# Shift and scale of the first layer as matrix products in four column groups, with two Q and K tiles run between the parts of V

## The chip, the cores and the metric

The kernel runs on one core of a Trainium2 chip. The metric is the device time of one execution in microseconds (us); of several runs the median counts.

## The reference

Two blocks of two layers each, on 256 tokens of width 1024, all in float32. Each layer computes six modulation vectors from a conditioning vector `c`, modulates a normed input, attends (or convolves), and runs a gated feed-forward. Only the start of the very first layer is touched by the change:

```python
c_act = jax.nn.silu(c)                                       # (1, 1024)
mod = jnp.einsum('bd,dm->bm', c_act, w_mod[i]) + b_mod[i]    # (1, 6 * 1024)
sh_a, sc_a, gt_a, sh_f, sc_f, gt_f = jnp.split(mod, 6, axis=-1)
h = rmsnorm(x, g_mix_pre[i]) * (1.0 + sc_a) + sh_a           # (256, 1024)
qkv = jnp.einsum('bsd,de->bse', h, w_qkv[i])                 # q, k, v: 1024 columns each
o = stick_breaking_attention(q, k, v)                        # 16 heads of 64
```

## The kernel before

Every product of activations with weights keeps float32 accuracy by a split: a weight chunk of 128x1024 comes in as `w`, ScalarE casts it to `wh` (the CAST rows), VectorE subtracts to get the rest `wl`, and three matmuls (`wh` with `hh`, `wl` with `hh`, `wh` with `hl`) make one product (`mm3`). A chunk that is loaded is 1 MB (two such halves) and lies in a slot of the class K8; there are three (`SLOTS`). SyncE issues all loads, in one queue.

The program is first recorded, then ordered by a list scheduler (`Rec.schedule`, with a planner's own costs), and put out in that order, engine by engine; on the chip each engine works through its own list in order and waits where an operand is not there.

The first layer begins with `first_values`. The width 1024 of the input is cut into eight tiles of 128 (`kt`), and these into four parts `q` of two tiles. For part `q`:

- `mods(q)` loads four 512 KB tiles `w` of `w_mod` (transposed: one output per partition) and VectorE reduces each against `c_act`, which stands on all partitions in `rows` (`dot`, the CUSTOM_DVE rows with their accumulator reads). `scale_of` makes (1 + scale) times gain. The columns are `msh_a` and `msc_a`.
- `first_tps` transposes the normed input `xn` of the part into `tps` (TensorE); VectorE (first tile) and ScalarE (second) apply scale and shift into `hf`, and that is split into `h0h`, `h0l` (parts 0 and 1) or `h1h`, `h1l` (parts 2 and 3).
- V is summed in four PSUM banks `acc`: 24 matmuls of 128x512 for each part, which this text calls V0 to V3. They need the part's `h` and the two halves of the part's V chunk.

After V3, `attention1` goes through eight tiles of Q and K (`project_t`, PSUM tile `qkps`, 48 matmuls of 128x256 each; QK0, QK1, ... here), then scores `z`, weights, transposes `atp` and outputs `op`. The reductions for the later modulation vectors run beside them on VectorE (`bg`). The order of the loads around the change: the four parts' `w_mod` tiles and V chunks in turn, then QK0, QK1, the first chunk of `w_o`, QK2.

Of the kernel before, what the change touches and what calls it, by code (L numbers as in the profile page):

```python
# [263 lines left out]
class Rec:  # L264
# [19 lines left out]
    def record(self, eng, fn, args, kw):  # L284
        op = Op()
        op.i, op.eng, op.fn, op.args, op.kw = len(self.ops), self.ENGINES[eng], fn, args, kw
        op.outs, op.deps, op.tiles, op.dma, op.act = [], {}, [], 0, 0
        outs = [kw[k] for k in ("out", "accum_out") if isinstance(kw.get(k), VAP)]
        ins = [v for k, v in kw.items() if k not in ("out", "accum_out") and isinstance(v, VAP)]
        pos = [a for a in args if isinstance(a, VAP)]  # L290
        if pos and "out" not in kw:
            outs.append(pos[0])
            pos = pos[1:]
        ins += pos
        if fn == "matmul" and not kw["start"]:
            ins.append(outs[0])
        for v in ins:
            self.access(op, v, False)
        for v in outs:
            self.access(op, v, True)  # L300
        if fn == "matmul" and kw["start"]:
            v = outs[0]
            for w in v.t.writes:
                if w[3] is not op and w[1] < v.parts[1] and w[2] > v.parts[0]:
                    op.deps.setdefault(w[3], 1)
        if self.after is not None:
            op.deps.setdefault(self.after, 1)
        for t in op.tiles:
            t.ops.append(op)
        op.cost = self.cost(op, outs, ins, args, kw)  # L310
        self.ops.append(op)
# [271 lines left out]
class Builder:  # L583
# [44 lines left out]
    def setup(self):  # L628

        nc, io = self.nc, self.io  # L630
        self.mhalf = self.const.tile([P, 16], F32, tag="mhalf", name="mhalf")
        nc.gpsimd.memset(self.mhalf, -0.5)
        self.cact = self.const.tile([P, 24], F32, tag="cact", name="cact")
        nc.sync.dma_start(out=self.cact, in_=self.io["vecs"][:, 0:24])
        self.eye = self.const.tile([P, P], F32, tag="eye", name="eye")
        nc.sync.dma_start(out=self.eye, in_=io["consts"][:, 0:P])
        self.vec = self.const.tile([P, NVEC], F32, tag="vec", name="vec")
        nc.sync.dma_start(out=self.vec[:, 0 : self.FIRST], in_=self.io["vecs"][:, 0 : self.FIRST])
        nc.scalar.activation(out=self.cact, in_=self.cact, func=AF.Silu)
        self.cb = {0: self.on_all_rows(self.cact[:, 0:8])}  # L640

    def setup_x(self):
# [311 lines left out]
    def values(self):  # L954
# [12 lines left out]
        self.bg(0.2)  # L967
        return self.evict_v(acc)

    def first_values(self):  # L970

        nc, io = self.nc, self.io
# [5 lines left out]
        def mods(q):  # L978
            for k in range(2):
                f = q * 2 + k  # L980
                i = len(self.plan)
                self.plan.append([("w_mod", 0, None, 1, a * D + f * P, D) for a in range(2)])
                for a, kind in enumerate(("sh_a", "sc_a")):
                    w = self.sb.tile([P, D], F32, name="w0")
                    nc.sync.dma_start(out=w, in_=io["wst"][i][:, a * D : (a + 1) * D])
                    if f + a == 0:
                        self.setup_x()
                    self.dot(w, self.cb[0], 0, 0, kind, f)
                self.scale_of(0, 0, "sc_a", f, 1)

        mods(0)
        xn = [self.normed(self.x[t], None, self.xe[t]) for t in range(2)]
        for q in range(4):
            w = self.w.load()
            tps = self.first_tps(xn, q)
            for k in range(2):
                kt = q * 2 + k
                a, b = self.modcols["sc_a"][:, kt : kt + 1], self.modcols["sh_a"][:, kt : kt + 1]
                h = self.sb.tile([P, 2, P], F32, name="hf")
                if k == 0:  # L1000
                    nc.vector.tensor_scalar(out=h, in0=tps[:, k], scalar1=a, scalar2=b, op0=ALU.mult, op1=ALU.add)
                else:
                    nc.scalar.activation(out=h, in_=tps[:, k], func=AF.Identity, scale=a, bias=b)
                hh, hl = self.hm(self.h, kt)
                nc.scalar.copy(hh, h)
                nc.vector.tensor_tensor(out=hl, in0=h, in1=hh.bitcast(F32), op=ALU.subtract)
            if q < 3:
                mods(q + 1)
# [4 lines left out]
        nc.after = nc.ops[-1]  # L1013
        self.setup_rest()
        nc.after = None
        return self.evict_v(acc)

    def first_tps(self, xn, q):
# [113 lines left out]
    def attention1(self, i):  # L1132
        nc = self.nc
        stick = i == 0
        vs = self.first_values() if stick else self.values()
        cum = None
        if stick:
            self.cprod = [self.sb.tile([P, 386], F32, tag=f"cp{k}", name=f"cp{k}") for k in range(2)]
            for cp in self.cprod:
                nc.gpsimd.memset(cp[:, 128:129], 1.0)  # L1140
                nc.gpsimd.memset(cp[:, 385:386], 1.0)
        else:
            cum = self.forget_cum()
        wo = Stream(self, [(("w_o", i, j * P, 2, 0, D),) for j in range(0, KT, 2)])
        qk, a, os_, w2 = {}, {}, {}, {}
        for it in range(KT + 2):
            if it < KT:
                w = self.w.take()
                ps = self.pmm.tile([P, 512], F32, tag="mm", name="qkps")
                for m in range(2):  # L1150
                    self.project_t(ps[:, m * S : (m + 1) * S], w[m], self.h)
# [409 lines left out]
    def run(self):  # L1561
# [93 lines left out]
```

## Time and profile before

| | us |
|---|---|
| median of 3 runs | 1354.19 (1352.99 to 1358.27) |
| the profiled execution, its own time | 1356.83 |
| its span, first to last instruction | 1355.0 |
| TensorE busy in the span | 1318.0 (97%) |
| VectorE busy | 1083.6 (80%) |
| ScalarE busy | 716.2 (53%) |

The profile is of one execution; its own time is 2.6 us above the median. A timeline row has the start, the duration, the engine, the operation with its output and inputs, the shape, how many alike were merged, and in brackets how long the engine had been idle and what ended that. A matmul's end is modelled, so the pace of TensorE is read from start to start of rows. PE is TensorE, PEld its weight loads, DVE VectorE, ACT ScalarE, SP SyncE. L544 is the line of the helper that records every operation, so rows are told apart by their tiles.

### The profile page before, as it was taken

The page shows a single profiled execution, that of the slowest core. Times are in us where ns is not written, and L with a number is a line of the kernel's source. Part 1 is how long each engine was busy: PE and PEld are TensorE (multiplying, and loading weights), DVE is VectorE, ACT ScalarE, POOL GpSimd, SP SyncE. Part 2 cuts the span into 40 slices and gives each one's busy share as a digit, 9 for nine tenths or more (in the row PEclk, how much of TensorE's full clock was granted, in tenths as well). Part 3 has the DMA queues.
Part 4 walks back from the last instruction along what each step waited for, and adds up shares of the span by engine and source line. Part 5 has one row for each costly group of instructions (what it writes and reads, how often), then busy time and mean ns, then how long its engine had stood idle before and what let it go on. Part 6 is the DMA issues. An engine that isn't in the chain of part 4 may idle for free.

```text
span 1355.0 us, 21985 instructions
## 1 busy us (share of the span) xinstructions
PE 1318.0 (97%) x8776; PEld 1178.4 (87%) x8776; DVE 1083.6 (80%) x1825; ACT 716.2 (53%) x1249; POOL 72.4 (5%) x102
## 2 busy tenths in 40 slices
PE   5999899999999999999999999899999999999998
PEld 3788799999898799999988777799999899899997
DVE  6888989899898499999799998886776898855542
ACT  3565655555656484556454567754444545744430
POOL 0000100000100000001033112100000000000000
PEclk9999999999999999999999999899999999999999
DMA  9857578887666256667544641576776688455520
GB/s 360 316 211 272 194 280 321 330 313 293 239 252 252 89 184 260 267 252 270 206 161 173 226 154 63 189 304 254 280 269 260 231 300 309 181 193 186 187 95 32
DMA packets 45320, 311.84 MB, mean 230 GB/s; under 512 B 5280, under 2 KB 5664, under 8 KB 8864
## 3 DMA queue, kind: packets, MB, share of 16 engines
q1 hardware_dynamic: 45216, 310.42, 61.3%
q8 instruction: 69, 1.13, 0.3%
q14 instruction: 35, 0.29, 0.1%
HBM read 309.35 MB, written 1.05 MB: 229 GB/s over the span
## 4 chain that ended last, share of the span: by engine, by line
PE 90%; DVE 6%; ACT 2%; issue 1%; DMA 0%; POOL 0%; SPq 0%; ACTq 0%; POOLq 0%
PE gu L544 34%; PE acc L544 30%; PE qkps L544 7%; PE fp L544 4%; PE cu L544 3%; PE z L544 2%; PE bb L544 2%; PE qps L544 2%; DVE w L544 2%; PE op L544 1%; DVE wl L544 1%; PE dop L544 1%; PE tps L544 1%; PE kc L544 1%; PE atp L544 1%
## 5 line engine op out<-in xcount | busy, mean ns | idle before, releaser
L544 DVE TENSOR_TENSOR wl<-w,wh 128x1024 fp32r<-128x1024 f32 x392 | 470.8, 1220 | 77.9 <-ACT wh L544 54.7
L544 ACT CAST wh<-w 128x1024 fp32r<-128x1024 f32 x392 | 402.4, 1049 | 98.8 <-DMA w<-in_wst_dram 56.7
L544 DVE CUSTOM_DVE_ANT_0 w<-w,rows,vec 128x1024 f32<-128x1024 f32 x192 | 242.4, 1278 | 9.9 <-DMA w<-in_wst_dram 9.6
L544 PE MATMUL gu<-h1h,wh 128*128 128x256 f32 x640 | 181.3, 283 | 0.0
L544 PE MATMUL gu<-h1h,wl 128*128 128x256 f32 x640 | 181.2, 283 | 0.0
L544 PE MATMUL gu<-h0h,wl 128*128 128x256 f32 x640 | 181.1, 283 | 0.0
L544 PE MATMUL gu<-h1l,wh 128*128 128x256 f32 x640 | 181.1, 283 | 0.0
L544 PE MATMUL gu<-h0l,wh 128*128 128x256 f32 x640 | 181.1, 283 | 0.0
L544 PE MATMUL gu<-h0h,wh 128*128 128x256 f32 x640 | 180.9, 283 | 0.0
L544 PE MATMUL acc<-wh,yh 128*128 128x512 f32 x352 | 137.6, 392 | 0.0
L544 PE MATMUL acc<-wl,yh 128*128 128x512 f32 x352 | 137.5, 391 | 0.0
L544 PE MATMUL acc<-wh,yl 128*128 128x512 f32 x352 | 135.3, 389 | 0.0
L544 PEld LDWEIGHTS gu<-h0l,wh 128*128 128x128 f32 x640 | 122.6, 192 | 2.2
L544 PEld LDWEIGHTS gu<-h0h,wh 128*128 128x128 f32 x640 | 122.5, 192 | 2.3
L544 PEld LDWEIGHTS gu<-h1l,wh 128*128 128x128 f32 x640 | 122.8, 192 | 0.1
L544 PEld LDWEIGHTS gu<-h1h,wh 128*128 128x128 f32 x640 | 122.8, 192 | 0.1
L544 PEld LDWEIGHTS gu<-h1h,wl 128*128 128x128 f32 x640 | 122.8, 192 | 0.0
L544 PEld LDWEIGHTS gu<-h0h,wl 128*128 128x128 f32 x640 | 122.6, 192 | 0.0
L544 DVE TENSOR_TENSOR y<-s,gu 128x256 f32<-128x256 f32 x80 | 33.5, 418 | 76.2 <-ACT s L544 76.2
L544 ACT ACTIVATE s<-gu 128x256 f32<-128x256 f32 x40 | 15.4, 385 | 138.0 <-PE gu L544 138.0
L544 PEld LDWEIGHTS acc<-wh,yl 128*128 128x128 f32 x352 | 66.1, 188 | 14.3
L544 PEld LDWEIGHTS acc<-wh,yh 128*128 128x128 f32 x352 | 66.3, 188 | 12.2 <-ACT yh L544 0.2
(364 smaller groups left out, 2690.4 us busy)
## 6 DMA issues: line engine op xcount, KB each, us to landing
w<-in_wst_dram SPq DMA_DIRECT2D x284, 1024.0 KB, 4.9
w<-in_wst_dram SPq DMA_DIRECT2D x16, 512.0 KB, 11.4
x<-in_x_dram SPq DMA_DIRECT2D x2, 512.0 KB, 6.6
cx<-in_ctx_dram SPq DMA_DIRECT2D x2, 512.0 KB, 6.3
out_dram<-x SPq DMA_DIRECT2D x1, 512.0 KB, 2.6
out_dram<-x SPq DMA_DIRECT2D x2, 256.0 KB, 2.0
cst<-in_consts_dram SPq DMA_DIRECT2D x1, 264.0 KB, 5.2
smalls<-in_smalls_dram SPq DMA_DIRECT2D x1, 256.0 KB, 5.2
```

The costliest lines, as they stand in the source:

```text
L544: fn(*[real(a) for a in op.args], **{k: real(v) for k, v in op.kw.items()})
```

## The change

Four things change, all in the first layer's first stage.

1. The 16 reductions of `mods` leave VectorE. `first_mods(q)` loads the same bytes of `w_mod`, now untransposed (rows of `c` on the partitions, 256 columns of shift and 256 of scale), and TensorE multiplies: for each of the four tiles, four matmuls with 32 equal columns of `c_act` as weights, each into its own 32 partitions of one PSUM tile `gv`. ScalarE copies `gv` to `gvs`; four matmuls against the column `four` (1 at partitions 0, 32, 64, 96) add the four groups and turn the row into columns; VectorE adds the bias and makes the scale, two columns at a time.
2. TensorE's instructions in this stage stand in the order in which the code writes them (`nc.serial`), not in the scheduler's.
3. QK0 and QK1 are run in parts between V's parts (`BETWEEN`, `project_part`), and their weight chunks are loaded between V's: V0, V1, QK0, V2, QK1, V3.
4. `setup_rest` (two small loads of constants) stands ahead of V2's chunk in the load queue instead of behind V3.

```diff
+        if self.serial is not None and op.eng == "PE":
+            if self.serial:
+                op.deps.setdefault(self.serial[-1], 1)
+            self.serial = [op]
...
+    def first_mods(self, q):
...
+        ps = self.pmm.tile([P, 512], F32, name="gv")
+        for a in range(2):
+            for kt in range(KT):
+                h, g = kt // 4, kt % 4
+                nc.tensor.matmul(
+                    ps[32 * g : 32 * g + 32, a * S : (a + 1) * S], lhsT=self.cact[:, kt : kt + 1].to_broadcast([P, 32]),
+                    rhs=ws[a, h][:, g * S : (g + 1) * S], start=h == 0, stop=h == 1,
+                )
+        gv = self.sb.tile([P, 512], F32, name="gvs")
+        nc.scalar.copy(gv, ps)
+        yield
+        for c in range(4):
+            nc.tensor.matmul(ps[:, c : c + 1], lhsT=gv[:, c * P : (c + 1) * P], rhs=self.four, start=True, stop=True)
...
+    BETWEEN = {1: ((0, (0, 1, 2, 3)),), 2: ((0, (4, 5)), (1, (0, 1, 2, 3, 4, 5))), 3: ((0, (6, 7)), (1, (6, 7)))}
...
             w = self.w.take(w)
             for t in range(2):
                 for k in range(2):
                     self.acc_mm(acc, t, self.hx(self.h, t, q * 2 + k), w[k], q + k == 0, q + k == 4)
...
+            if q < 3:
+                next(mods[q + 1])
+                tps = self.first_tps(xn, q + 1)
+            parts = [(j, kt) for j, kts in self.BETWEEN.get(q, ()) for kt in kts]
...
+            for n, (j, kt) in enumerate(parts):
+                if n == 2 and q < 3:
+                    next(mods[q + 1])
+                self.project_part(self.early_qk[j], qkw[j], (kt,))
...
-                specs += self.value_specs(i) + self.qk_specs(i)
+                v, qk = self.value_specs(i), self.qk_specs(i)
+                specs += v + qk if i else [v[0], v[1], qk[0], v[2], qk[1], v[3]] + qk[2:]
```

The instructions move on three engines. First TensorE between V0 and V1. Before, the last matmuls of V0 (`wl_239`, `wh_213`) are followed at once by V1's (`wh_246`, `wl_254`):

```order
L544 MATMUL acc_217<-wl_239,h0h_200 128x512
L544 MATMUL acc_217<-wh_213,h0l_204 128x512
L544 MATMUL acc_219<-wl_239,h0h_200 128x512
L544 MATMUL acc_219<-wh_213,h0l_204 128x512
L544 MATMUL acc_211<-wh_246,h0h_200 128x512
L544 MATMUL acc_215<-wh_246,h0h_200 128x512
L544 MATMUL acc_217<-wh_246,h0h_200 128x512
```

Now (V0's last two, then the products for part 1, its transposes, the four sums, then V1's first three, with `wh_267` and `wl_280`):

```order
L551 MATMUL acc_248<-wl_228,h0h_214 128x512
L551 MATMUL acc_248<-wh_222,h0l_224 128x512
L551 MATMUL gv_258<-w_44_111,cact_83 32x256 x4
L551 MATMUL gv_258<-w_45_113,cact_83 32x256 x4
L551 MATMUL gv_258<-w_46_115,cact_83 32x256 x4
L551 MATMUL gv_258<-w_47_117,cact_83 32x256 x4
L551 MATMUL tps_277<-eye_85,xn_173 128x128
L551 MATMUL tps_277<-eye_85,xn_181 128x128
L551 MATMUL gv_258<-four_143,gvs_286 128x1 x4
L551 MATMUL acc_220<-wh_267,h0h_214 128x512
L551 MATMUL acc_220<-wl_280,h0h_214 128x512
L551 MATMUL acc_220<-wh_267,h0l_224 128x512
```

The products for part 1 stand behind all of V0, and nothing stands between the four sums and V1. Between V1 and V2, V2 and V3 the pieces of QK0 and QK1 fill that place.

Second, VectorE at the same place. Before, a reduction (the rows named ISA) and the rest of V0's chunk (`wl_239`) are followed by the scale and by `hf`:

```order
L544 ISA w_44_117,raw_176<-w_44_117,rows_148,vec_91 128x1024
L544 ISA raw_176 128x1
L544 TENSOR_TENSOR wl_239<-w_37_109,wh_213 128x1024
L544 SCALAR_TENSOR_TENSOR msc_a_184<-raw_176,vec_91 128x1
L544 TENSOR_SCALAR hf_242<-tps_169,msc_a_184,msh_a_156 128x256
L544 TENSOR_TENSOR wl_254<-w_49_119,wh_246 128x1024
L544 TENSOR_TENSOR h0l_204<-hf_242,h0h_200 128x2x128
```

Now the two biased sums, then the two rests of QK0's chunk (`wl_300`, `wl_305`) on either side of the scale, then `hf`:

```order
L551 TENSOR_TENSOR msh_a_204<-gv_258,vec_91 128x2
L551 TENSOR_TENSOR raw_206<-gv_258,vec_91 128x2
L551 TENSOR_TENSOR wl_300<-w_58_121,wh_291 128x1024
L551 SCALAR_TENSOR_TENSOR msc_a_208<-raw_206,vec_91 128x2
L551 TENSOR_TENSOR wl_305<-w_58_121,wh_302 128x1024
L551 TENSOR_SCALAR hf_307<-tps_277,msc_a_208,msh_a_204 128x256
L551 TENSOR_TENSOR h0l_224<-hf_307,h0h_214 128x2x128
```

The reductions are gone, and both rests of QK0 stand ahead of the `hf` that V1 waits for. Third, ScalarE. Before, the cast of V2's first half (`wh_289`) stands ahead of the casts of part 2's `h`:

```order
L544 CAST h0h_200<-hf_257 128x2x128
L544 CAST wh_289<-w_61_129 128x1024
L544 CAST h1h_299<-hf_292 128x2x128
L544 ACTIVATE hf_304<-tps_174,msh_a_156,msc_a_184 128x256
```

Now, from the copy of part 1's products to the cast of V2's second half (`wh_291`, `wh_302` are QK0's halves, `wh_406`, `wh_412` V2's):

```order
L551 COPY gvs_286<-gv_258 128x512
L551 CAST wh_291<-w_58_121 128x1024
L551 CAST wh_302<-w_58_121 128x1024
L551 CAST h0h_214<-hf_307 128x2x128
L551 ACTIVATE hf_312<-tps_277,msh_a_204,msc_a_208 128x256
L551 CAST h0h_214<-hf_312 128x2x128
L551 COPY gvs_361<-gv_341 128x512
L551 CAST h1h_400<-hf_393 128x2x128
L551 ACTIVATE hf_402<-tps_358,msh_a_204,msc_a_208 128x256
L551 CAST wh_406<-w_63_237 128x1024
L551 CAST h1h_400<-hf_402 128x2x128
L551 CAST wh_412<-w_63_237 128x1024
```

The casts of QK0's halves now stand behind the copy of part 1's products, and V2's first cast stands behind part 2's `h`. From the first feed-forward on the order is the same as before, but for a few rows at its start.

## Rows read from the trace of the kernel before

**Rows 1.** The page's first line and its busy line: us busy, share of the span, instructions, engine by engine.

```profile
span 1355.0 us, 21985 instructions
PE 1318.0 (97%) x8776; PEld 1178.4 (87%) x8776; DVE 1083.6 (80%) x1825; ACT 716.2 (53%) x1249; POOL 72.4 (5%) x102
```

**Rows 2.** The view by stretches of 10 us: the stretch and its length, then busy us (and instructions) of PE, PEld, DVE, ACT and POOL, then TensorE's granted clock (1.00 is full speed), the busy share of the DMA engines and GB/s.

```profile
30.00:40.00 10.00, 7.38 (x32) 5.55 (x30) 10.00 (x18) 3.97 (x6) 0.00 (x0) 1.00 1.01 410
40.00:50.00 10.00, 7.38 (x26) 5.91 (x26) 8.50 (x14) 4.80 (x9) 0.00 (x0) 0.83 0.56 205
50.00:60.00 10.00, 10.00 (x78) 9.69 (x77) 6.94 (x8) 7.86 (x11) 0.00 (x0) 1.00 0.85 326
```

**Rows 3.** What TensorE waited for: us in total, times, the longest. The first two rows from the stretch 0 to 60 us, the last two from 60 to 170 us (the largest of five there, 4.7 us together).

```profile
PE acc L544 <- DVE wl L544: 7.1, 3, 2.6
PE acc L544 <- ACT wh L544: 2.4, 1, 2.4
...
PE fp L544 <- ACT h0h L544: 1.9, 4, 0.7
PE tps L544 <- DVE u L544: 1.8, 1, 1.8
```

**Rows 4.** Timeline: V's first matmuls; QK0's first; QK1's last and the first scores.

```profile
18.39 2.07 PE L544 MATMUL acc<-wh,h0h 128*128 128x512 f32 x4 [2.38 <-ACT wh L544]
...
51.75 0.28 PE L544 MATMUL qkps<-h0h,wh 128*128 128x256 f32 x1
...
63.14 0.28 PE L544 MATMUL qkps<-h1h,wl 128*128 128x256 f32 x1
63.35 0.49 PE L544 MATMUL z<-qk 64*128 64x128 f32 x4
```

**Rows 5.** Timeline of ScalarE: the first casts of the chunks of V1, V2 and V3, each started by its load's landing.

```profile
24.01 1.04 ACT L544 CAST wh<-w 128x1024 fp32r<-128x1024 f32 x1 [4.42 <-DMA w<-in_wst_dram]
31.61 1.04 ACT L544 CAST wh<-w 128x1024 fp32r<-128x1024 f32 x1 [2.97 <-DMA w<-in_wst_dram]
39.19 1.05 ACT L544 CAST wh<-w 128x1024 fp32r<-128x1024 f32 x1 [2.19 <-DMA w<-in_wst_dram]
```

**Rows 6.** Timeline of TensorE: float32 products with 64 columns of weights (`op`), in two column groups in turn. Each call of the code leaves two rows. First all four calls of a pair of heads together (two of 256 columns, two of 128), then one call of 256 columns alone; the row behind each shows when the next matmul began.

```profile
73.77 0.87 PE L544 MATMUL op<-at,v 128*64 128x256 f32 x8
74.57 0.39 PE L544 MATMUL qkps<-h0l,wh 128*128 128x256 f32 x1
...
83.22 0.65 PE L544 MATMUL op<-at,v 128*64 128x256 f32 x2
83.80 0.39 PE L544 MATMUL qkps<-h0h,wl 128*128 128x256 f32 x1
```

**Rows 7.** The same for the whole array: four transposes of 128x128, and four float32 products with 128 columns of weights and 128 columns streamed (`dop`), each with the row behind it; last, eight weight loads for transposes early in the span.

```profile
780.33 0.66 PE L544 MATMUL dtp<-eye,p 128*128 128x128 f32 x4
780.74 0.49 PE L544 MATMUL acc<-wh,h0h 128*128 128x512 f32 x1
...
782.00 1.15 PE L544 MATMUL dop<-dv,dat 128*128 128x128 f32 x8
782.90 0.47 PE L544 MATMUL acc<-wh,h0l 128*128 128x512 f32 x1
...
11.22 1.57 PEld L544 LDWEIGHTS tps<-eye,xn 128*128 128x128 f32 x8 [6.28 <-DVE xn L544]
```

**Rows 8.** Timeline: V matmuls at full clock, three and three; V matmuls at half clock.

```profile
47.65 0.86 PE L544 MATMUL acc<-wh,h1h 128*128 128x512 f32 x3
48.34 0.85 PE L544 MATMUL acc<-wl,h1h 128*128 128x512 f32 x3
...
43.75 0.63 PE L544 MATMUL acc<-wl,h1h 128*128 128x512 f32 x1
44.18 0.63 PE L544 MATMUL acc<-wh,h1l 128*128 128x512 f32 x1
```

**Rows 9.** Prices of the small steps, from the timeline: ScalarE's copy of 512 columns out of PSUM, VectorE's rest of a half chunk, scale and `hf`, ScalarE's cast of `hf` and its own `hf`; and the page's group of the reductions (busy us, mean ns).

```profile
4.53 0.59 ACT L544 COPY rows<-rowps 128x512 f32<-128x512 f32 x1 [1.84 <-PE rowps L544]
33.10 1.22 DVE L544 TENSOR_TENSOR wl<-w,wh 128x1024 fp32r<-128x1024 f32 x1
34.24 0.15 DVE L544 SCALAR_TENSOR_TENSOR msc_a<-raw,vec 128x1 f32<-128x1 f32 x1
34.31 0.54 DVE L544 TENSOR_SCALAR hf<-tps,msc_a,msh_a 128x256 f32<-128x256 f32 x1
34.88 0.41 ACT L544 CAST h1h<-hf 128x256 fp32r<-128x256 f32 x1 [2.22 <-DVE hf L544]
35.19 0.56 ACT L544 ACTIVATE hf<-tps,msh_a,msc_a 128x256 f32<-128x256 f32 x1
...
L544 DVE CUSTOM_DVE_ANT_0 w<-w,rows,vec 128x1024 f32<-128x1024 f32 x192 | 242.4, 1278 | 9.9 <-DMA w<-in_wst_dram 9.6
```

**Rows 10.** The view by stretches again (columns as in rows 2), around a wait of TensorE from 40.1 to 42.7 us.

```profile
34.30:40.20 5.90, 5.73 (x24) 4.43 (x24) 5.90 (x13) 3.13 (x5) 0.00 (x0) 1.00 0.99 406
40.20:42.70 2.50, 0.00 (x0) 0.00 (x0) 2.50 (x8) 0.04 (x1) 0.00 (x0) 1.00 0.09 33
42.70:46.20 3.50, 3.47 (x8) 2.82 (x9) 3.10 (x5) 2.96 (x6) 0.00 (x0) 0.51 0.67 225
```

**Rows 11.** The page's DMA issues: the 1 MB chunks, KB each, median us from issue to landing.

```profile
w<-in_wst_dram SPq DMA_DIRECT2D x284, 1024.0 KB, 4.9
```

More of the change, by code (lines that the diff above doesn't have):

```diff
@@ L639, in setup @@
         nc.scalar.activation(out=self.cact, in_=self.cact, func=AF.Silu)
+        self.four = self.const.tile([P, 1], F32, tag="four", name="four")
+        nc.vector.tensor_reduce(
+            out=self.four, in_=self.eye.rearrange("p (a d) -> p a d", a=4)[:, :, 0], axis=AX.X, op=ALU.add
+        )
         self.cb = {0: self.on_all_rows(self.cact[:, 0:8])}
@@ L968, in values @@
         return self.evict_v(acc)
+    def first_mods(self, q):
+        nc = self.nc
+        i = len(self.plan)
+        self.plan += [[("w_mod", 0, 0, KT, a * D + q * S, S)] for a in range(2)]
+        ws = {}
+        for a in range(2):
+            for h in range(2):
+                ws[a, h] = self.sb.tile([P, D], F32, name="w0")
+                nc.sync.dma_start(out=ws[a, h], in_=self.io["wst"][i + a][:, h * D : (h + 1) * D])
+                if q + a + h == 0:
+                    self.setup_x()
+        yield
+        ps = self.pmm.tile([P, 512], F32, name="gv")
+        for a in range(2):
+            for kt in range(KT):
[3 more added lines that the diff above has]
+                    rhs=ws[a, h][:, g * S : (g + 1) * S], start=h == 0, stop=h == 1,
+                )
+        gv = self.sb.tile([P, 512], F32, name="gvs")
+        nc.scalar.copy(gv, ps)
+        yield
+        for c in range(4):
+            nc.tensor.matmul(ps[:, c : c + 1], lhsT=gv[:, c * P : (c + 1) * P], rhs=self.four, start=True, stop=True)
+        f = 2 * q
+        for a, (kind, out) in enumerate((("sh_a", self.modcols["sh_a"]), ("sc_a", self.raw["sc_a"]))):
+            nc.vector.tensor_tensor(
+                out=out[:, f : f + 2], in0=ps[:, 2 * a : 2 * a + 2], in1=self.v(f"b00{kind}", f, 2), op=ALU.add
+            )
+        self.scale_of(0, 0, "sc_a", f, 2)
+        yield
@@ new lines, in first_h @@
+    def first_h(self, tps, q):
+        nc = self.nc
+        for k in range(2):
+            kt = q * 2 + k
+            a, b = self.modcols["sc_a"][:, kt : kt + 1], self.modcols["sh_a"][:, kt : kt + 1]
+            h = self.sb.tile([P, 2, P], F32, name="hf")
+            if k == 0:
+                nc.vector.tensor_scalar(out=h, in0=tps[:, k], scalar1=a, scalar2=b, op0=ALU.mult, op1=ALU.add)
+            else:
+                nc.scalar.activation(out=h, in_=tps[:, k], func=AF.Identity, scale=a, bias=b)
+            self.split_to(self.hm(self.h, kt), h)
@@ L976, in first_values @@
         self.raw["sc_a"] = self.sb.tile([P, 8], F32, name="raw")
[L978 to L991, printed above, removed]
+        mods = [self.first_mods(q) for q in range(4)]
+        nc.serial = []
+        next(mods[0])
+        next(mods[0])
+        w = self.w.load()
         xn = [self.normed(self.x[t], None, self.xe[t]) for t in range(2)]
+        tps = self.first_tps(xn, 0)
+        next(mods[0])
+        self.first_h(tps, 0)
+        qkw, self.early_qk = {}, {}
         for q in range(4):
[L994 to L1006, printed above, removed]
+            if q in (1, 2):
+                late = self.w.load()
             if q < 3:
-                mods(q + 1)
+                next(mods[q + 1])
+                nextw = self.w.load()
+            if q == 2:
+                self.setup_rest()
             w = self.w.take(w)
@@ L1012, in first_values @@
                     self.acc_mm(acc, t, self.hx(self.h, t, q * 2 + k), w[k], q + k == 0, q + k == 4)
[L1013 to L1015 removed]
+            if q < 3:
+                next(mods[q + 1])
+                tps = self.first_tps(xn, q + 1)
+            parts = [(j, kt) for j, kts in self.BETWEEN.get(q, ()) for kt in kts]
+            if q in (1, 2):
+                qkw[q - 1] = self.w.take(late)
+                self.early_qk[q - 1] = self.pmm.tile([P, 512], F32, name="qkps")
+            for n, (j, kt) in enumerate(parts):
+                if n == 2 and q < 3:
+                    next(mods[q + 1])
+                self.project_part(self.early_qk[j], qkw[j], (kt,))
+            if q < 3:
+                if len(parts) <= 2:
+                    next(mods[q + 1])
+                self.first_h(tps, q + 1)
+                w = nextw
+        nc.serial = None
         return self.evict_v(acc)
@@ L1147, in attention1 @@
             if it < KT:
[L1148 to L1151, printed above, removed]
+                ps = self.early_qk.pop(it, None)
+                if ps is None:
+                    w = self.w.take()
+                    ps = self.pmm.tile([P, 512], F32, tag="mm", name="qkps")
+                    for m in range(2):
+                        self.project_t(ps[:, m * S : (m + 1) * S], w[m], self.h)
                 qk[it] = self.sb.tile([P, 512], F32, tag="qk", name="qk")
```

14 lines of the change are left out of this document (12 added, 2 removed).

## Prediction

> **What bounds the kernel now.** The page first [rows 1]: TensorE is busy for 1318.0 us of the span of 1355.0. Only 37 us are idle, and the question is where. The stretches [rows 2] answer it: TensorE has 7.38 us of work in each of the stretches 30 to 40 and 40 to 50, and 10.00 from 50 to 60. VectorE is full in the first of them, and the DMA engines move 410 GB/s. The waits [rows 3] name the rest: until 60 us TensorE waits 7.1 us for VectorE's `wl` and 2.4 for the first cast; between 60 and 170 us it waits 4.7 us in all, and the two largest items, 1.9 and 1.8, belong to the step from the attention to the feed-forward. So the span is TensorE's own work, plus holes nearly all of which lie in the first 50 us. What the change is worth is therefore one difference: when TensorE has V, QK0 and QK1 behind it. Before, V begins at 18.39, QK0 at 51.75, and QK1 is done at 63.35 [rows 4]. In those 45 us it has 96 V matmuls, three of them in 0.69 us at full clock [rows 8], that is 0.23 each or 21.9 us (at 0.228), and 96 QK matmuls from 51.75 to 63.35, 0.12 each or 11.5. The remaining 11.5 us are holes and half clock. The change can fill at most these, and has to pay out of them for all that it adds to TensorE.
>
> **What leaves VectorE.** Sixteen reductions of 1.28 us [rows 9], 20.5 us. They set the pace of V before: each of the three waits for `wl` had reductions ahead of it in VectorE's queue. The added small steps there (two sums and a scale for each part, at most 0.15 each [rows 9]) are under 2 us.
>
> **When the data land.** The same 8 MB of `w_mod` are loaded. Three chunk times, 24.01, 31.61 and 39.19 [rows 5], lie 3 MB apart, so 1 MB takes 2.53 us. Before V1's chunk the queue is unchanged: V1 lands at 24.0, and part 0's four `w_mod` tiles, 4 MB ahead of it, at 24.0 - 10.1 = 13.9. From there on QK0 lands at 26.5, part 2's tiles at 31.6, part 3's at 36.7, then the two small loads (0.46 MB), V2 at 40.4, QK1 at 43.0, V3 at 45.5. Part 1's tiles are there at 21.5. Of these only part 0's tiles hold up the path below.
>
> **What TensorE gains in work.** One part's products are 16 calls of 256 columns in four groups of 32. No row of before shows four groups; the nearest show two [rows 6]. A call of 256 columns alone holds the array from 83.22 to 83.80, 0.58. Two of 256 and two of 128 in two groups take 73.77 to 74.57, 0.80. With c for a call of 256, half of it for 128, and s for going in and out: side by side 1.5c + s = 0.80 and c + s = 0.58, so c = 0.44 and s = 0.14. One after the other would be 3c + s = 0.80, so c = 0.11; but four whole-array calls of 128 columns take 0.90 [rows 7], 0.22 each, which is c = 0.44. So two groups do run side by side. Bounds for a part: four at a time 4 x 0.44 + 0.14 = 1.9; two at a time 8 x 0.44 + 0.14 = 3.7; one at a time 7.2. I take 1.9, since the rows show no loss at two.
>
> The Trainium skill, "TensorEngine Tiling (Array Packing)", Tiling Modes, has four independent tiles for 128 rows and 32 columns, but says that changing the mode drains the engine; the trace agrees with the second in the 0.14. The skill's "TensorE: Matmul & The Clock Gate", Part 3, gives 2.38 times for three column tiles; by that share, an estimate from this page, a part would take 2.4 and the sum below would be 1.4 us higher.
>
> The four sums are weight loads with one column streamed: at most the 0.90 of four whole-array calls [rows 7], at least the 0.41 of four transposes [rows 7]; I take 0.90, since the loads are of the same kind. The four transposes, 0.41, now stand on the path too.
>
> **The path, part by part.** Ends of one engine and starts of the next lie within 0.05 us in the rows; I add 0.2 for the last result of TensorE.
>
> Start of V0. The last tile lands at 13.9; the last four products, at the half pace of the start (V's first four matmuls take 2.07 [rows 4], where three take 0.69 later [rows 8]), 0.9 and 0.2: 15.0. Copy 0.59: 15.6, while the transposes run until 15.9. The four sums are eight weight loads at that pace, 1.57 [rows 7], and 0.2: 17.7. Sums and scale 0.4, `hf` 0.54, cast 0.41 [rows 9]: V0 begins at 19.2, 0.8 later than before. Its first half needs `wl`, which stands behind `hf` (1.22, third matmul at 20.3), runs at half pace (0.43 each [rows 8]) and waits for the second half's `wl` until 22.4; at full pace from there, V0 ends at 26.5. That is 7.3 us where the matmuls alone are 5.5.
>
> Between V0 and V1. Products 1.9 and 0.2: 28.6. Copy: 29.2. Four sums 0.9 and 0.2: 30.35. Now VectorE's order bites: after the two biased sums it must make the rest of QK0's first half, whose cast stands behind the copy on ScalarE (30.3), 1.14 from start to start [rows 9], then the scale, then the second rest, 1.14, then `hf` 0.54: 33.5. Cast: V1 begins at 34.0. TensorE stands still for 3.8 us after the four sums; its longest wait for `wl` before was 2.6 [rows 3]. A hole of 2.6 us, 40.1 to 42.7, left it at a granted clock of 0.51, the 1.2 GHz of its two levels, for about 3.2 us; another, which ended at 34.3, did not, as the 1.00 of the stretch behind it shows [rows 10]. I count the lower level after V1's hole: 1.6 us lost. V1 is 5.5 + 1.6 and ends at 41.1.
>
> Between V1 and V2. Products 1.9, transposes 0.4, two pieces of QK0 (12 x 0.12 = 1.44, they hide the copy), four sums 0.9, with the result at 45.95. Two more pieces run until 47.2. The chain beside them is longer: sums and scale 0.4, `hf` 0.57, cast 0.46, ScalarE's `hf` 0.58, and only then V2's first cast, 1.05, though its chunk landed at 40.4: V2 begins at 49.0, a hole of 1.8. Its second matmul waits for `wl`, 1.22, until 50.25; the other 23 take 5.3 and wait 0.15: 55.65. QK1's own casts come behind, done by 54.2.
>
> Between V2 and V3. Products 1.9, transposes 0.4, two pieces of QK0 1.44, four sums 0.9, six pieces of QK1 36 x 0.12 = 4.3: 64.6. What is queued ahead of part 3's `hf`: on ScalarE and VectorE the splits of the first `w_o` chunk, which can be issued only when V2's chunk is split (51.8) and lands 4.9 later [rows 11], at 56.7, and of QK2, issued at 54.2 and landed at 59.1. With copy, casts and rests in their order `hf` is cast by about 63.4, so 1.2 us before V3 wants it. These pieces are the cover; without them V3 would wait as V1 does. V3 is 5.5, with two matmuls of QK2 in it 5.7: 70.35. The last 24 QK matmuls, 2.9: 73.2.
>
> **The sum.** 73.2, less 0.24 for QK2's two, against 63.35 before: 9.6 us later. By kinds: later start 0.8; three times products, transposes and sums 3 x 3.2 = 9.6; waits and half clock in V0 1.8, before V1 4.3 (with the copy), V1's clock 1.6, V2 2.9; together 21.0, against the 11.5 of holes that are gone. Nothing gives it back: TensorE hardly waits between 63 and 149 us, so a VectorE that is ahead does not shorten it, and the waits behind that are a chain which the change leaves alone. Against the profiled execution: 1356.8 + 9.6 = 1366.4; its time is 2.6 above the median, so for the median I say **1363.8**.
>
> **The rivals.**
>
> *The groups do not run four at a time.* Two at a time cost 3 x 1.8 = 5.4 more on the path: 1369. One at a time 3 x 5.3 = 15.9: 1380. For it: no row shows four. Against it: two show no loss [rows 6]. Chance 0.13.
>
> *TensorE stays at full clock.* Not slower by what can be told. The products for part 0 keep it running from 11 to 17 us, so V0 might start at full clock (ten matmuls at 0.23 instead of 0.43, of which its waits leave some 1.3), and V1's hole might not lower it (1.6): 9.6 - 2.9 = 6.7, 1360.9. It decides at V1: a granted clock of 1.0 in V1's first 3 us. For it: the hole before 34.3 passed [rows 10]. Against it: this one is 3.8. Chance 0.17.
>
> *No holes at all.* If the small steps went ahead of QK0's rests and V2's casts, TensorE would run through from 19.2: 21.9 + 11.5 + 9.6 = 62.2 at best, 1.2 earlier than before: 1353. It decides on VectorE between the biased sums and the scale. Against it: an engine keeps its order. Chance 0.07. This is also the floor, and the reason why a gain of 0.5% would need something that no row shows: 0.03.
>
> **The numbers.** 0.5% of this kernel, 6.8 us, is about what a measurement can tell from no change. The forecast has 0.60; its own range is +6 to +14 us (no hole before V2; sums and products at the dear end, a late `hf` before V3). I give 0.50 of it to slower by more than 6.8, 0.10 to less. Slower: 0.50 + 0.13 + 0.03 of the clock's case = 0.66. Within: 0.10 + 0.14 + 0.07 = 0.31. Faster: 0.03. The range goes from 1356, which leaves out the case without holes, to 1372, which takes in two groups at a time and leaves out one at a time.
>
> **What would show it.** Right: V0 starts near 19, V1 near 34 after a hole of 3 to 4 us that ends on a cast behind VectorE's `wl`; V2 starts on a cast near 49; the four `gv` tiles of a part take about 2 us; the first scores begin near 73.5; no reductions on VectorE before 60 us; after that all rows shifted alike. Wrong: `gv` at 4 us or more a part (first rival), V1 at 0.23 a matmul from its start (second), no hole before V1 (third), or a stretch between 75 and 150 us that is shorter than before, which would mean that VectorE held the attention though no wait showed it.

## The result, and the profile after the change

The kernel became slower: a median of 1366.43 us (1363.68 to 1368.27, 4 runs) beside 1354.26 of before (1352.99 to 1358.27), ratio 1.0083, 95% interval 1.0056 to 1.0110. The profiled execution took 1366.57 us, 9.7 more than that of before. The forecast for the median was 1363.8. The page's first line and its busy line:

```profile
span 1364.8 us, 22266 instructions
PE 1331.8 (98%) x8936; PEld 1185.4 (87%) x8936; DVE 1065.6 (78%) x1798; ACT 719.5 (53%) x1253; POOL 73.5 (5%) x102
```

Beside [rows 1]: VectorE has 18 us less to do, TensorE 14 us more, and the span is 9.8 longer. The stretches that answer to [rows 2], with the same columns:

```profile
30.00:40.00 10.00, 6.32 (x20) 5.09 (x21) 4.20 (x9) 3.14 (x5) 0.00 (x0) 0.71 1.03 411
40.00:50.00 10.00, 9.56 (x81) 7.54 (x79) 1.33 (x5) 1.42 (x4) 0.00 (x0) 0.95 0.39 161
50.00:60.00 10.00, 8.21 (x59) 5.58 (x60) 7.51 (x9) 7.23 (x10) 0.00 (x0) 1.00 0.55 191
```

VectorE, full from 30 to 40 us before, is now busy for 4.2 of 10 and for 1.3 in the next stretch; TensorE still has holes, and from 30 to 40 a granted clock of 0.71. Its waits from 0 to 80 us, which answer to the first two of [rows 3]:

```profile
PE acc L551 <- ACT h0h L551: 5.2, 2, 3.7
...
PE acc L551 <- ACT wh L551: 1.5, 1, 1.5
PE acc L551 <- DVE wl L551: 0.8, 1, 0.8
```

V's waits add up to 7.5 us; before they were 9.5. So the holes moved and shrank by 2 us in all. TensorE's timeline shows where; these rows answer to [rows 4], and in brackets stands the wait ahead of a row and what ended it:

```profile
14.36 1.08 PE L551 MATMUL gv<-w,cact 128*32 128x256 f32 x8 [0.36 <-DMA w<-in_wst_dram]
...
19.60 0.80 PE L551 MATMUL acc<-wh,h0h 128*128 128x512 f32 x1 [1.58 <-ACT h0h L551]
...
27.39 1.93 PE L551 MATMUL gv<-w,cact 128*32 128x256 f32 x32
29.25 0.66 PE L551 MATMUL tps<-eye,xn 128*128 128x128 f32 x4
30.03 1.05 PE L551 MATMUL gv<-four,gvs 128*128 128x1 f32 x8
34.73 0.79 PE L551 MATMUL acc<-wh,h0h 128*128 128x512 f32 x1 [3.65 <-ACT h0h L551]
...
43.28 1.93 PE L551 MATMUL gv<-w,cact 128*32 128x256 f32 x32
...
51.03 0.49 PE L551 MATMUL acc<-wh,h1h 128*128 128x512 f32 x1 [1.46 <-ACT wh L551]
52.29 0.50 PE L551 MATMUL acc<-wl,h1h 128*128 128x512 f32 x1 [0.77 <-DVE wl L551]
...
57.84 1.93 PE L551 MATMUL gv<-w,cact 128*32 128x256 f32 x32
...
66.85 0.40 PE L551 MATMUL acc<-wh,h1h 128*128 128x512 f32 x1
...
76.14 0.49 PE L551 MATMUL z<-qk 64*128 64x128 f32 x4
```

Read it as a walk. V0 from 19.60, part 1's products at 27.39, the transposes 1.86 us later, the four sums, then nothing for 3.65 us until V1. Between V1 and V2 the wait is for ScalarE's cast of V2's chunk; V3 starts without a wait. Seven matmuls of QK2 (0.84 us) stand ahead of the scores at 76.14, so V, QK0 and QK1 are done at 75.30, 11.95 later than before. What VectorE does in the hole before V1:

```profile
31.19 0.16 DVE L551 TENSOR_TENSOR msh_a<-gv,vec 128x2 f32<-128x2 f32 x1 [3.35 <-PE gv L551]
31.26 0.15 DVE L551 TENSOR_TENSOR raw<-gv,vec 128x2 f32<-128x2 f32 x1
31.36 1.22 DVE L551 TENSOR_TENSOR wl<-w,wh 128x1024 fp32r<-128x1024 f32 x1
32.50 0.15 DVE L551 SCALAR_TENSOR_TENSOR msc_a<-raw,vec 128x2 f32<-128x2 f32 x1
32.57 1.22 DVE L551 TENSOR_TENSOR wl<-w,wh 128x1024 fp32r<-128x1024 f32 x1
33.70 0.54 DVE L551 TENSOR_SCALAR hf<-tps,msc_a,msh_a 128x256 f32<-128x256 f32 x1
```

Both rests of QK0's chunk, 2.28 us start to start, stand between the sums and `hf`. And the stretches of the hole, of V1 at the low clock, and of V1's end:

```profile
31.10:34.70 3.60, 0.00 (x0) 0.00 (x0) 3.06 (x6) 1.19 (x3) 0.00 (x0) 0.92 1.02 409
34.70:41.00 6.30, 6.27 (x15) 4.91 (x16) 1.15 (x3) 0.85 (x2) 0.00 (x0) 0.51 1.04 418
41.00:43.30 2.30, 2.30 (x15) 1.63 (x13) 0.00 (x0) 0.00 (x0) 0.00 (x0) 1.00 1.00 417
```

### The profile page after: what moved, and what is told of

Its sections match the earlier page's. It is cut to its first block, busy times and chain, and to the rows that moved or that the text cites. A ratio compares the mean times of both kernels' runs of the same rounds, so it can differ in the third digit from the quotient of the medians.

```text
span 1364.8 us, 22266 instructions
## 1 busy us (share of the span) xinstructions
PE 1331.8 (98%) x8936; PEld 1185.4 (87%) x8936; DVE 1065.6 (78%) x1798; ACT 719.5 (53%) x1253; POOL 73.5 (5%) x102
## 4 chain that ended last, share of the span: by engine, by line
PE 91%; DVE 5%; ACT 2%; DMA 1%; issue 1%; POOL 1%; SPq 0%; ACTq 0%; DVEq 0%; POOLq 0%
PE gu L551 34%; PE acc L551 31%; PE qkps L551 7%; PE fp L551 3%; PE cu L551 3%; PE z L551 2%; PE bb L551 2%; PE qps L551 2%; PE op L551 1%; DVE wl L551 1%; PE tps L551 1%; PE dop L551 1%; PE kc L551 1%; DMA w<-in_wst_dram 1%; PE atp L551 1%; PE dz L551 1%
## 5 line engine op out<-in xcount | busy, mean ns | idle before, releaser
L551 DVE CUSTOM_DVE_ANT_0 w<-w,rows,vec 128x1024 f32<-128x1024 f32 x176 | 222.6, 1278 | 3.3 <-DMA w<-in_wst_dram 3.0
L551 PEld LDWEIGHTS acc<-wh,yh 128*128 128x128 f32 x352 | 66.3, 188 | 12.3 <-ACT yh L551 0.2
```

The costliest lines, as they stand in the source:

```text
L551: fn(*[real(a) for a in op.args], **{k: real(v) for k, v in op.kw.items()})
```

## Experiments

"Scores" is the start of the first scores in the profiled execution, less 0.12 us for each QK2 matmul that the order puts ahead of them; it reads finer than the medians, since the runs of one kernel scatter by 2 to 5 us. The ratio is that to the kernel before on the same chip, whose median was 1354.26 beside the change, 1356.29 beside the next four kernels, 1355.15 beside the four from "two holes" on, and 1356.00 beside the last. The intervals of the change, small steps first, products alone, filler and two holes overlap: their times don't tell them apart, so those runs are read by the rows of the stage.

| kernel | median us | ratio, 95% interval | scores | span |
|---|---|---|---|---|
| before | 1354.26 | 1 | 63.35 | 1355.0 |
| change | 1366.43 | 1.0083 (1.0056 to 1.0110) | 75.30 | 1364.8 |
| one group | 1384.25 | 1.0204 (1.0186 to 1.0222) | 92.68 | 1382.8 |
| small steps first | 1363.42 | 1.0055 (1.0035 to 1.0076) | 71.87 | 1361.7 |
| products alone | 1363.37 | 1.0059 (1.0038 to 1.0079) | 72.29 | 1361.1 |
| filler in the hole | 1363.83 | 1.0059 (1.0042 to 1.0076) | 72.92 | 1362.0 |
| two holes | 1363.99 | 1.0065 (1.0051 to 1.0080) | 71.09 | 1362.5 |
| no holes | 1359.00 | 1.0033 (1.0021 to 1.0046) | 67.25 | 1357.2 |
| pieces alone | 1360.30 | 1.0036 (1.0023 to 1.0049) | 66.01 | 1358.9 |
| rests on GpSimd | 1368.62 | 1.0102 (1.0089 to 1.0116) | 73.90 | 1366.4 |
| pieces, mended | 1355.11 | 0.9998 (0.9989 to 1.0008) | 59.21 | 1352.3 |

**One column group.**

```
-  ps[32 * g : 32 * g + 32, a * S : (a + 1) * S], ... start=h == 0, stop=h == 1,
+  ps[0:32, a * S : (a + 1) * S], ... start=kt == 0, stop=kt == KT - 1,
```

> The change, with all 16 products of a part in one group of 32 columns (one after the other on the same 32 columns of the array) and four sums over 32 rows in place of 128. My theory: the products of parts 1 to 3 stand on TensorE's path and ran four at a time (1.86 us a part); one at a time they take 16 x 0.44 + 0.14 = 7.2, so V, QK0 and QK1 end 3 x 5.3 = 15.9 us later and part 0's last products at half pace some 3 us more, less a little cover: 1366.4 + 16 to 19 = 1382 to 1385. Rival (the products already ran one at a time, or are hidden behind VectorE): 1366, no change.

```profile
28.31 7.09 PE L551 MATMUL gv<-w,cact 128*32 128x256 f32 x32
35.34 0.66 PE L551 MATMUL tps<-eye,xn 128*128 128x128 f32 x4
```

The same 16 products take 7.03 us from start to start, where the change takes 1.86. So four groups do run side by side, 3.8 times as fast as one. The scores come 17.4 us later than in the change and the span is 18.0 longer: TensorE's queue up to the scores is the path, and what is put on it here arrives at the end almost whole. The first rival of the prediction is out.

**Small steps first.**

```
+  nc.after = last_h if q == 1 else None
   qkw[q - 1] = self.w.take(late)
+  nc.after = None
```

> The change, with QK0's two casts and rests made to wait for part 1's h, so that the small steps (biased sums, scale, hf, cast) go ahead of them. My theory: the hole before V1 shrinks from 3.65 us to about 1.4 and V1 starts at 32.4 in place of 34.7; a hole of 1.4 does not lower the clock, so V1 takes 5.5 in place of 8.55; V2 starts near 46 and everything behind comes 2.3 + 3.0 = 5.3 us earlier: 1361. If the lower clock has another cause than the hole (for instance the narrow products and sums ahead of it), V1 stays at a granted clock of 0.51 and only 2.3 are won: 1364. Rival (TensorE's queue up to the scores does not set the end): 1366, no change.

The hole before V1 fell to 1.60 us, V1 began at 32.23, and the order of VectorE is thereby shown to be what made 2 us of the 3.65. But only 3.1 us of span were won, not 5.3, and 1.0 of these lies ahead of V0, which began at 18.61 in place of 19.60 because part 0's last tile landed that much earlier; no row shows why. Stretches: the hole, V1, V2's first part, V2's end (columns as in rows 2).

```profile
30.60:32.20 1.60, 0.02 (x1) 0.00 (x0) 0.93 (x4) 0.43 (x2) 0.00 (x0) 1.00 1.02 410
32.20:37.90 5.70, 5.67 (x24) 4.36 (x24) 3.21 (x4) 2.75 (x4) 0.00 (x0) 1.00 1.04 411
...
47.40:51.30 3.90, 3.90 (x10) 3.09 (x11) 3.90 (x4) 3.40 (x4) 0.00 (x0) 0.56 0.44 132
51.30:54.40 3.10, 3.10 (x14) 2.25 (x12) 1.70 (x2) 0.00 (x0) 0.00 (x0) 1.00 1.00 365
```

V1 ran at full clock, as expected; now V2 had the lower one, behind waits of 1.91 and 0.77 us, though behind 1.46 and 0.77 in the change it had not.

**Products alone.** `BETWEEN = {}`, no early chunks, QK0 and QK1 left to the planner behind V.

> The products on TensorE alone: no pieces of QK0 and QK1 between V's parts; QK0 and QK1 run behind V3 as before the change, and their chunks are loaded behind V3's. My theory: three holes of 1.4 us (sums, scale, hf, cast) before V1, V2 and V3, none of which lowers the clock, V1 from 32.4, V2 from 43, V3 from 53.5, QK1 done at 70.5 in place of 75.3: 1366.4 - 4.8 = 1361.6. That would mean that the pieces as ordered cost more than they hide. If the clock falls after holes of 1.4 too, up to 3 us each more: 1364 to 1370. Rival (the pieces are what hides the small steps, as their place suggests): slower than the change by 3 to 5 us, 1370.

Without the pieces the kernel is 3.7 us shorter in span than the change, where I expected 4.8; 0.9 of it is V0's earlier start (18.73). V1 and V2 started at 32.15 and 43.10 as forecast, each behind 1.60 us; V2 then had a clock of 0.77 over its 7.3 us. Before V3 the planner by itself put 36 QK0 matmuls, so this last gap is not as I drew it. Small steps first, which keeps the pieces, has the same time (medians 1363.42 and 1363.37), so these times don't show that the pieces as such cost anything, or that they hide anything.

**Filler in the hole.**

```
+  for n in range(14):
+      nc.tensor.matmul(fill, lhsT=self.hx(self.h, 0, 0)[0], rhs=w[0][0][:, 0:512], start=n == 0, stop=n == 13)
```

> The change, with 14 matmuls of 128x512 added in the hole before V1, whose result is not used (V1's first half chunk by part 0's h, 14 x 0.23 = 3.2 us). My theory: the hole is what lowers the clock for V1; kept busy, V1 runs at a granted clock of 1.0 and takes 5.5 us in place of 8.55, while it starts when it did (34.7): 1366.4 - 3.0 = 1363.4. If the clock falls for what ran before (narrow products, weight loads), V1 stays at 8.5 us and the time at 1366; if the filler itself delays V1, V1 starts later than 34.8.

The hole with the filler, and V1:

```profile
31.40:35.20 3.80, 3.48 (x16) 2.54 (x15) 3.07 (x7) 1.39 (x3) 0.00 (x0) 1.00 1.02 407
35.20:40.90 5.70, 5.69 (x24) 4.36 (x25) 1.13 (x3) 0.83 (x2) 0.00 (x0) 1.00 1.04 421
```

14 useless matmuls more, and the span is 2.8 us shorter, the median 2.6. V1 took 5.69 us in place of 8.55, its start 0.5 later. The narrow products and sums ran ahead of it as in the change, so it is the idle time that goes with the lower clock. That is one profile; how much weight one bears, the last two runs tell. The kernel's four runs point the same way: their mean granted clock over the whole span was 0.996 to 0.999, that of the change's four 0.995 to 0.996.

**Two holes.** As small steps first, with QK1's split behind part 2's `h` as well, and part 2's `hf` behind V2's second cast.

> The second experiment (QK0's split behind part 1's h) with one more order: part 2's hf waits for V2's second cast, so that both casts of V2's chunk, which landed long before, run while ScalarE is idle. My theory: the hole before V2 (1.91 and 0.77 us there) shrinks to 0.3 to 0.5, V2 starts near 44.3 in place of 46.1, and since no hole of more than 1.6 is left, V2 runs at full clock, 5.5 us in place of 8.3: V2 ends near 50.2 in place of 54.4 and the kernel is 4.2 us faster than in the second experiment, 1363.4 - 4.2 = 1359.2. If the low clock in V2 came from something else than this hole, V2 takes 7 us: 1361. If V3's cover is lost instead (its chunk or part 3's hf late), part of it comes back as a wait before V3.

The expected 1359.2 was missed (1363.99), in a way worth seeing. VectorE, between part 2's sums and its `hf`:

```profile
44.24 0.15 DVE L551 TENSOR_TENSOR raw<-gv,vec 128x2 f32<-128x2 f32 x1
44.42 0.16 DVE L551 SCALAR_TENSOR_TENSOR msc_a<-raw,vec 128x2 f32<-128x2 f32 x1
44.49 0.28 DVE L551 CAST bf<-cst 128x256 bf16<-128x256 f32 x1
44.70 2.35 DVE L551 TENSOR_TENSOR wl<-w,wh 128x1024 fp32r<-128x1024 f32 x2
46.97 0.54 DVE L551 TENSOR_SCALAR hf<-tps,msc_a,msh_a 128x256 f32<-128x256 f32 x1
```

The casts came early, and drew V2's two rests ahead of `hf`: the same trap as in the change, one part later. V2 waited 2.40 us in one piece. And V1, behind the same hole of 1.60, took 7.3 us this time.

**No holes.**

```
-  BETWEEN = {1: ((0, (0, 1, 2, 3)),), 2: ((0, (4, 5)), ...
+  BETWEEN = (((0, (0, 1)),), ((0, (2, 3)),), ((0, (4, 5)), ...
```

The entries are, in turn, what stands between V0 and V1, V1 and V2, V2 and V3, and behind V3. The rest of the edit, not shown, puts QK0's split ahead of part 1's copy, the sums ahead of the pieces, and V2's chunk ahead of part 3's tiles.

> The third rival of the prediction, built: the products and sums stay on TensorE, but in every gap stands work. QK0's split runs ahead of part 1's copy (its chunk lands at about 26.5), two pieces of QK0 behind part 1's sums and two behind part 2's, V2's chunk is loaded ahead of part 3's tiles and split early. My theory (TensorE's own work is the floor): from V0's start at 18.6 to 19.6 without a hole of more than 0.4 us, V1 at 32, V2 at 42, V3 at 57 or earlier in the order, first scores near 65.5 in place of 76.1 of the change and 63.35 of before: 1366.4 - 10 = 1356.5, which is 1 to 3 us behind the kernel before. If it comes out below 1352, the change's added work on TensorE is not the floor that the prediction took it for.

TensorE's waits from 17 to 60 us, and the stretch 27 to 54:

```profile
PE acc L551 <- ACT h0h L551: 1.6, 1, 1.6
PE qkps L551 <- DVE wl L551: 0.5, 1, 0.5
PE acc L551 <- DVE wl L551: 0.2, 1, 0.2
```

```profile
27.00:54.00 27.00, 26.61 (x220) 20.26 (x220) 13.48 (x22) 12.60 (x18) 0.00 (x0) 1.00 0.84 337
```

The 1.6 lies before V0. From part 1's products to part 3's TensorE runs through at full clock, and still the kernel is 1.0033 times as long as before (1.0021 to 1.0046); 1356.5 was expected, 1359.00 measured. Scores came 1.8 us later than expected, in small pieces. So the floor stands: what the change puts on TensorE's path, about 3.1 us for each of three parts (1.86, 0.41 and 0.80 from start to start in the change) and V0's later start, takes up nearly all of the 11.5 us that it can fill.

**Pieces alone.** The reductions back on VectorE; VectorE's, ScalarE's and TensorE's order up to V3 written by hand.

> The other half of the change alone: the shift and scale stay on VectorE as 16 reductions (as in the kernel before), and only the pieces of QK0 and QK1 run between V's parts, with VectorE's and ScalarE's order written by hand (a V part's rests ahead of the next part's reductions, QK0's rests ahead of part 2's, QK1's in the middle of part 3's). My theory: the 11.5 us of holes before the change are filled with QK work that must be done anyway, while VectorE gets only 4.6 us more ahead of V3: V3 starts near 49 and the first scores come near 58 in place of 63.35: 1354.3 - 5 = 1349. Rival: VectorE, full until 47 us, is held up further by each added rest, so that V2 and V3 come later by what the pieces save: no change against before, 1354. Second rival: the scores come earlier, and the attention behind them waits for VectorE or loads instead: 1352 to 1354 with a wait between 60 and 100 us that was not there before.

Slower than before, but by my own order: TensorE's waits for `wh` were 8.0 us in three, since I had put each chunk's casts behind the part's `h` on ScalarE, and VectorE stood idle 1.91 us for transposes that I had put behind V0. So it tells nothing on the rivals of this expectation.

**Rests on GpSimd.** `nc.gpsimd.tensor_tensor` for the four rests of QK0 and QK1, the same hand order, but with QK1's pieces behind V3.

> As the pieces alone, but the four rests of QK0's and QK1's chunks are made by GpSimd, which is idle here, and QK1's pieces run behind V3. My theory: VectorE is relieved of 4.6 us, V3 starts near 45 to 46, TensorE has no hole from V2 on, first scores near 56: 1347. Rival: GpSimd's rest takes so long (no row shows one; VectorE's takes 1.22 us) that QK0's pieces wait, or it slows VectorE's work beside it: then V1 to V2 shows a wait for wl of GpSimd, or VectorE's rests take more than 1.22, and the time is that of the pieces alone or worse, 1349 to 1356.

GpSimd's rests, and VectorE beside them and just behind:

```profile
31.45 6.00 POOL L551 TENSOR_TENSOR wl<-w,wh 128x1024 fp32r<-128x1024 f32 x2 [19.98 <-ACT wh L551]
```

```profile
31.82 3.39 DVE L551 CUSTOM_DVE_ANT_0 w<-w,rows,vec 128x1024 f32<-128x1024 f32 x1
...
35.15 3.39 DVE L551 CUSTOM_DVE_ANT_0 w<-w,rows,vec 128x1024 f32<-128x1024 f32 x1
...
38.47 1.27 DVE L551 CUSTOM_DVE_ANT_0 w<-w,rows,vec 128x1024 f32<-128x1024 f32 x1
```

A reduction takes 1.27 us alone and 3.39 while GpSimd makes a rest, so two rests moved away (2.3 us of VectorE) cost it 4.2. The Trainium skill, "SBUF — State Buffer", SBUF: two separate sides, says that a VectorE operation with two SBUF inputs and a GpSimd operation that reads SBUF exclude each other for a whole instruction; these rows agree, since both reductions that start while GpSimd works are 2.1 us longer than the one that starts after it. If so, the 6.0 us of GpSimd's two rests hold a wait for VectorE as well; what one takes undisturbed no run shows. The kernel took 1368.62, more than even the rival allowed. Its span is 7.5 us longer than that of the pieces alone, but QK1's pieces stand elsewhere, so not all of this is shown to be GpSimd's.

**Pieces, mended.** Casts of a V chunk ahead of the part's `h`, transposes of the next part ahead of V.

> The pieces alone once more, with two mistakes of the hand order taken out that the trace of the first try showed: the transposes for the next part now run ahead of a V part and not behind it (VectorE stood idle for them, 1.9 us before V1), and ScalarE casts a V chunk ahead of the part's h and not behind it (TensorE waited 8.0 us for those casts). My theory: V1 starts near 27.4, V2 near 39, V3 near 50, first scores near 58.7 in place of 63.35 of the kernel before; the hole before V1 is still 2.5 us and may cost 1.5 to 3 us of clock: 1350 to 1353. Rival (VectorE, full until 47 us before, is the bound, and each rest of QK0 and QK1 ahead of V3 delays it by as much as the pieces save): V3 later than 52, scores at 62 to 64, 1354.

Scores at 59.21, within 0.5 of the expectation and 4.1 earlier than before: here the pieces do fill holes. TensorE's waits from 60 to 170 us:

```profile
PE tps L551 <- DVE u L551: 3.3, 1, 3.3
```

The wait at the step to the feed-forward grew from 1.8 [rows 3] to 3.3, and at the transposes behind it 1.9 of the 4.1 us are left (149.92 against 151.82). Behind this longer wait the clock fell, too: from 152.2 to 158.4 us TensorE had a granted clock of 0.50, some 3 us lost, where the profile of before had 1.00 (its own fall comes at 165.6 us and cost 1.7). The stretch with it, columns as in rows 2:

```profile
140.00:160.00 20.00, 14.35 (x67) 11.98 (x65) 16.92 (x39) 12.05 (x32) 3.94 (x4) 0.83 0.36 150
```

The span is 2.7 us shorter, between one profile of each. Over 12 runs against 17 of before the ratio is 0.9998 (0.9989 to 1.0008): not told from no change. This best version is no proven gain.

**The change, profiled again.**

> The changed kernel itself, unaltered, profiled a second time. Question: does the lower clock behind a hole depend on the program or on the execution? In the first profile V1, behind a hole of 3.65 us, ran at a granted clock of 0.51 for 6.3 us and took 8.55 us. If the program decides, V1 takes 8.5 us again, within 0.2; if the execution does, V1 takes anything from 5.6 to 8.6 us here, with the same hole of 3.6 to 3.7 us.

```profile
35.55 0.79 PE L551 MATMUL acc<-wh,h0h 128*128 128x512 f32 x1 [3.66 <-ACT h0h L551]
...
42.81 1.93 PE L551 MATMUL gv<-w,cact 128*32 128x256 f32 x32
```

The same hole, 3.66, but V1 took 7.26 us in place of 8.55: the low clock lasted about 3.3 us. This time V2 had it too (8.35 us in place of 6.81). Span 1366.3, scores at 76.36.

**Small steps first, profiled again.**

> The second experiment (small steps first), unaltered, profiled a second time. In its first profile V1 ran at full clock behind a hole of 1.60 us and V2 at a granted clock of 0.56 for 3.9 us behind holes of 1.91 and 0.77 us; another kernel with the same V1 and the same hole of 1.60 had V1 at 0.77. If the program decides, V1 takes 5.7 us and V2 8.3 us again; if the execution does, one of them differs by 1 us or more.

The waits were the same to 0.01 us (1.60; 1.91 and 0.77), and the clock the other way round: V1 took 7.3 us, V2 6.7, where the first profile had 5.7 and 8.3. So one program with the same holes has the lower clock in one execution and not in another. These second profiles were taken on another chip than the first ones of small steps first, but the chip isn't needed for it: 17 runs of the kernel before on one chip had a mean granted clock of 0.992 to 0.996. The nine at 0.993 or less took 1356.0 to 1357.9 us, the eight at 0.994 or more 1352.8 to 1355.8. Much of the scatter of that kernel's runs goes with this clock.

## Why the prediction was right

| step | predicted | measured |
|---|---|---|
| part 0's last tile | 13.9 | 14.36 |
| V0 begins | 19.2 | 19.60 |
| V0 ends, part 1's products | 26.5 | 27.39 |
| products of a part | 1.9 | 1.86 |
| hole before V1 | 3.8 | 3.65 |
| V1 begins | 34.0 | 34.73 |
| V1 ends | 41.1 | 43.28 |
| V2 begins | 49.0 | 51.03 |
| V2 ends | 55.65 | 57.84 |
| V3 begins, no wait | 64.6 | 66.85 |
| QK1 done | 72.96 | 75.30 |
| later than before, at this point | 9.6 | 11.95 |
| later than before, at the end | 9.6 | 9.8 |

The number came out closer than the working deserves. Between the two profiles the forecast was 9.6 and the result 9.7; between the medians it is 12.2, with an interval of 7.6 to 14.9, since the profiled execution of before was 2.6 above its median and that of the change was not.

- **Four groups side by side.** 1.9 worked out from two groups of `op` [rows 6], 1.86 measured. One group gave 7.03. The estimate of 2.4 by the share in the Trainium skill ("TensorE: Matmul & The Clock Gate", Part 3) is not what these rows show.
- **The order on VectorE.** The two rests of QK0 ahead of `hf` were read from the order alone, and the 3.8 from the prices [rows 9]. Undone, the hole fell to 1.60.
- **V2's casts behind part 2's `h`.** From V1's end to V2's start 7.9 predicted, 7.75 measured, with the two waits in the places named.
- **V3's cover held**: its `h` was cast by 65.1, 1.8 us before it was wanted; 1.2 predicted.
- **The clock in V1** is the one term that was mis-sized: 1.6 predicted, 3.0 in this profile (8.55 less 5.55). The same program in a second execution lost 1.7. My one row [rows 10] was one draw from something that varies; I should have kept both ends, nothing and 3, for each hole and not for V1 alone. The rest of the 2.3 us by which the walk ran late is V0's start (0.4) and length (0.5). From the third to the tenth, V0's matmuls are 0.43 apart, as at half clock, though the view gives a granted clock of 1.00 there (19.6 to 23.8 us): for this stretch the pace is read from the starts.
- **"Nothing gives it back"** was out by 2.2 us in these two profiles, which happened to cancel the clock in V1: that is luck. 11.95 at the scores are 11.64 at the transposes for the feed-forward, 10.4 from the middle of the feed-forward on (a `rowps` row at 236.52 against 226.17) and 9.8 at the end. At the first of these the wait of 1.8 for `u` [rows 3] is gone, but the matmul behind it waits longer for `h0h`, and there the lag is 12.3 again. The change, then before:

```profile
163.46 1.03 PE L551 MATMUL tps<-eye,u 128*128 128x128 f32 x8
165.94 0.38 PE L551 MATMUL fp<-wh,h0h 128*128 128x256 f32 x1 [1.44 <-ACT h0h L551]
...
151.82 1.06 PE L544 MATMUL tps<-eye,u 128*128 128x128 f32 x8 [1.78 <-DVE u L544]
153.62 0.39 PE L544 MATMUL fp<-wh,h0h 128*128 128x256 f32 x1 [0.73 <-ACT h0h L544]
```

Behind the attention's last products the order now holds 58 matmuls of the output projection, where before it held 42 and in the mended pieces 32 (wait 3.3); the chain to `u` runs beside them. That fits the three, but no run changed this number alone, and the no-holes kernel (43, wait 0.2) does not fit by the number alone. The feed-forward itself gives back 1.9, and about half of that goes with the clock of one execution. The stretches from 160 to 180 us, before and change:

```profile
160.00:180.00 20.00, 18.99 (x140) 18.21 (x140) 16.26 (x26) 14.88 (x28) 0.02 (x1) 0.91 0.61 221
160.00:180.00 20.00, 16.32 (x113) 14.32 (x113) 19.11 (x37) 17.30 (x35) 3.38 (x3) 1.00 0.51 167
```

The profile of before ran there at 0.91, the change at 1.00. In the change's second profile, at 0.91 in this stretch, 12.4 of its 13.0 us at the scores are left in the middle of the feed-forward: it gave back 0.65 where the first gave back 1.6. The last 0.6 goes at about 880 us; that and what stands ahead of `u` stay open.
- **Where the holes of before lie.** "Nearly all of which lie in the first 50 us" is too much: of the 37 us in which TensorE was idle, 19.4 lie before 50 us, 4.6 between 150 and 170, and most of the rest behind 860. The sum does not rest on it, since it compares the same stretch in both kernels.
- **The floor** of the third rival was 62.2 at best; built, the scores came at 67.25 and the span was 2.2 us longer than before. 2.4 of the difference of 5.0 is V0, which took 7.86 us for 5.5 us of matmuls; the 62.2 had it run through.

## What to carry to other kernels

Before moving work off a full engine, add up what the receiving engine gains on its own path: here 3.1 us for each part against 11.5 us of holes in all left nothing to win in any of the orders tried. A short chain that another engine waits for must be read in the order of every engine it crosses, and filling work that is ready earlier is what slips ahead of it; the experiment that forced casts forward fell into the hole it was to close. The cheaper half of the change, filling the holes and leaving the reductions, got TensorE 4.1 us ahead at the scores, lost about half of that at the next chain, and ended with no gain that could be told from no change. And one profile on each side is not enough for a difference of 2 us: executions of one program differ by as much in the clock alone.

## What was not expected of the hardware

- The lower clock behind a wait differs between executions of one program: behind 3.65 us V1 ran at it for 6.3 us once and for about 3.3 once; behind 1.60 us it did or did not; a V2 behind 2.40 us did not. The shortest single wait ahead of it in this stage was 1.58 (V0 of no holes); two short ones in a row, 0.95 and 0.76, went ahead of it in pieces alone. In the kernel before it came at 165.6 us behind four waits of 0.23 to 0.50. With the hole filled it did not come, in the one profile there is.
- A reduction on VectorE slows from 1.27 to 3.39 us beside GpSimd's subtraction of the same size. Two such subtractions take 6.0 us there, where VectorE's take 1.22 each.
